# Soft-routed experts on one core: B22 loaded block by block, the second pair's reloads reordered, and the B11 sums moved in the program text

## The chip, the core and the metric

The kernel runs on one core of one Trainium2 chip. Its time is the device time of one execution in microseconds (us). The kernel before takes 1434.25 us, the median of 3 runs (1434.05 to 1435.16). The profile shown here is one further execution of the same program, with a span of 1434.2 us.

## What is computed

```python
batch, seq, hidden, n_experts, expert_hidden = 16, 512, 512, 8, 2048
probs = softmax(router_logits)                      # over the 8 experts
output = zeros(batch, seq, expert_hidden)
for e in range(8):
    output += probs[:, :, e:e+1] * (x @ expert_weights[e])
```

Every token goes through every expert, and the softmax of its logits weights the results. Written as one product, the output is Z times W: Z has 8192 rows (tokens) and 8 x 512 = 4096 columns, where column block e is x times the token's probability of expert e; W stacks the eight weight matrices to 4096 x 2048.

## The kernel before

The product Z W is cut into 2 x 2 blocks: token blocks of 256 rows are even or odd, experts are the first or the last four, output columns the first or the last 1024. Seven block products (numbered 1 to 7) then stand for eight, at the price of sums and differences of blocks, which VectorE makes. The weight blocks are B11, B12, B21 and B22, each of four tiles `w` of 128 x 4096 f16 (1 MB); the list `BLOCKS` names the four tiles. Products 1, 5, 2 and 4 are cut once more in the same way by `sub_product` (its seven inner products are the `prod(p, ...)` below, and its weights are the four tiles and the "inner sums" of them). Their results go to DRAM, product 4 into the output and products 1, 2 and 5 into `kept`. The last stage goes once over 16 pairs of row blocks (`for q in range(NI)`), makes products 6, 7 and 3, and reads `kept` back.

All helpers record their instructions on one line: L142 is every matmul of `mm`, L122 every two-operand VectorE operation of `tt`, L136 every DMA issued by GpSimd (`pool`), L133 every DMA issued by SyncE (`sp`). The program is written with a scheduling layer. It keeps VectorE and ScalarE instructions in the order of the text where `pinned[0]` is true; the others it may place elsewhere in their engine's order:

```python
    pinned = [True]
    def dve(i):
        note(i)
        if pinned[0]:
            tc.keep_in_program_order(i)
    def tt(o, a, b, op):
        dve(nc.vector.tensor_tensor(out=o, in0=a, in1=b, op=op))
```

The inner sums of a weight block are four operations on VectorE, each one tile from another:

```python
    def inner_sums(b, t3=None):
        t3 = t3 or b[0, 1]
        w = {1: b[0, 0], 2: b[1, 0], 3: b[1, 1], 7: t3}
        def step(p, x, y):
            if p not in w:
                w[p] = new_w()
            tt(w[p], x, y, SUB)
        return w, [lambda: step(5, b[0, 1], b[0, 0]), lambda: step(6, b[1, 1], w[5]),
                   lambda: step(4, w[6], b[1, 0]), lambda: step(7, b[1, 1], b[0, 1])]
```

The start of the kernel makes product 1 of the first row blocks directly (`z0`), and meanwhile the softmax of all tokens and the operands of the next two row blocks (numbers 4 and 6, `xp1`), whose probabilities are spread over the partitions by a matmul of `ones` with a diagonal matrix `d`:

```python
    def early_xp1(j, d):
        ...
        for c in range(C):
            mm(ps[:, ds(c * P, P)], xs0[:, j, ds(c * P, P)], ident, c == 0, c == C - 1)
        evacuate(xp1[t][0][:, :, rows], ps.rearrange("p (c t) -> p c t", c=C), 0)
        ps = bank()
        mm(ps, ones, d.rearrange("p e t -> p (e t)"), True, True)
        evacuate(xp1[t][1][:, :, rows], ps.rearrange("p (e t) -> p e t", e=HE), 1)
    ...
    for n in range(2):
        ps = [bank() for _ in range(4)]
        for e in range(HE):
            ...
            for c in range(C):
                for j in range(4):
                    mm(ps[j], z0[j][:, e, c], b11[e // 2, n][:, e % 2 * C + c, :],
                       e + c == 0, e == HE - 1 and c == C - 1)
            if n == 1:
                for j in ((4, 5), (6, 7), (), ())[e]:
                    early_xp1(j, ds_[j - 4])
                if e == 1:
                    sums[0]()
        for j in range(4):
            o = half()
            act(nc.scalar.copy(o, ps[j]))
            sp(kept[1][j // 2][n].rearrange("(p j) m -> j p m", j=2)[j % 2], o)
        if n == 0:
            ph0.append(early_p(1))
            softmax_of_all()
            ds_ = [diag_j(j) for j in range(4, 8)]
            w, sums = inner_sums(b11, new_w())
    ...
    pinned[0] = False
    sub_product(1, 0, P1, w, weights_of_t1(), 1,
                xp1, (sums[1], sums[3], sums[2]))
```

`sub_product` makes the operands of its first row blocks, then calls `rest`, then multiplies:

```python
            a11, a12 = (mul(*xp[0], e0, 2, 0, HQ) for e0 in (0, 2))
            a21, a22 = (mul(*xp[1], e0, 2, 0, HQ) for e0 in (0, 2))
            ...
            s1 = new(a21, a22, ADD)
            s2 = new(s1, a11, SUB)
            s4 = new(a12, s2, SUB)
            tt(a21, a11, a21, SUB)
            for make in rest:
                make()
            ...
                r1 = keep(prod(1, "x"))
                put(0, 0, prod(2, "b"), r1, ADD)
                r5 = keep(prod(5, "q"))
                r2 = keep(prod(6, "x", False))
                put(0, 1, prod(3, "q", False), r2, ADD)
                ...
```

The last stage, cut to the parts that the change touches:

```python
        def load_kept(self, j):
            tn = QUARTERS[j]
            self.m1[tn] = from_kept(1, self.q, *tn, "m")
            self.m5[tn] = from_kept(5, self.q, *tn, "v")
        def c11(self, j):
            tn = QUARTERS[j]
            m2 = from_kept(2, self.q, *tn, "m")
            tt(m2, self.m1[tn], m2, ADD)
            self.put(0, 0, tn, m2)
    ...
        xs, vs = [], []
        for j, tn in enumerate(QUARTERS):
            if j > 1:
                rows.load_kept(j)
            x = bank()
            act(nc.scalar.copy(x, rows.m1[tn]))
            if o10 and j == 0:
                o10()
            if j > 1 or q == 1:
                rows.c11(j)
            ...
            plain(x, 6, w6, tn, False)          # 16 matmuls onto the kept product 1
            v = half("u")
            tt(v, x, rows.m5[tn], ADD)
```

Here L626 is `act(nc.scalar.copy(x, rows.m1[tn]))`, and L595 is the GpSimd queue's store in `put`. `"m"` has five buffers, `"v"` four. The four tiles of B22 (`w3`) are needed by product 3 of q = 0, after 4 x 16 matmuls of product 6 and as many of product 7.

Of the kernel before, what the change touches and what calls it, by code (L numbers as in the profile page):

```python
# [32 lines left out]
def kernel(  # L33
# [38 lines left out]
    BLOCKS = ((0, 0), (1, 0), (0, 1), (1, 1))  # L72
# [41 lines left out]
# [4 lines that stand above are left out]
# [17 lines left out]
    def pool(o, i):  # L135
        note(nc.gpsimd.dma_start(out=o, in_=i))  # L136

    def bank():
        return psum.tile([P, NB], f32, name="ps", tag="ps")
# [8 lines left out]
    def new_w():  # L148
        return wpool.tile([P, K8, NB], f16, name="w", tag="w")

    def cast_w(q, kn, e, t, parts=1):
        k, n = kn
        for c in range(0, C, C // parts):
            pool(t[:, ds(e * C + c, C // parts), :],
                 expert_weights[(q // 10 - 1) * HE + 2 * k + e, ds(c * P, C * P // parts),
                                ds((q % 10 - 1) * NH + n * NB, NB)].rearrange("(c p) n -> p c n", p=P))

    def load(what, kn, gate=True):
        t = new_w()
        if gate:  # L160
            dve(nc.vector.memset(t.rearrange("p (e c) n -> p e c n", e=2)[:, :, 0, 0:2], 0.0))  # L161
        if (what, kn) in stored:
            pool(t, stored[what, kn])
        else:
            for e in range(2):
                cast_w(what, kn, e, t)
        return t
# [5 lines left out]
# [12 lines that stand above are left out]
    def inner_weights(b):  # L185
        w, sums = inner_sums(b)
        sums[0]()
        yield
        sums[1]()
        sums[2]()  # L190
        yield
        sums[3]()
        return w
# [72 lines left out]
    def diag_e(e):  # L266
        return diag(ph0[0][:, e].unsqueeze(2))
# [11 lines left out]
    xp1 = [[xpool.tile([P, C, HQ], f16, name=name, tag="x") for name in ("xT", "pT")] for t in range(2)]  # L279
# [73 lines left out]
    def half(use="any"):  # L353
        return h_tile([P, NB], f32, use)
# [87 lines left out]
# [3 lines that stand above are left out]
            if n == 0 and e < 2:  # L445
                early_z0(e + 2, ds_[e + 2])
                if e == 0:
                    ds_.append(diag_e(3))
# [4 lines that stand above are left out]
            if n == 1:  # L453
                for j in ((4, 5), (6, 7), (), ())[e]:
                    early_xp1(j, ds_[j - 4])
                if e == 1:
                    sums[0]()
        for j in range(4):
            o = half()
            act(nc.scalar.copy(o, ps[j]))  # L460
# [7 lines that stand above are left out]
    def weights_of_t1():  # L468
        b = {}
        for i, kn in enumerate(BLOCKS):  # L470
# [7 lines left out]
    x_new.extend((4 + 2 * t, xp1[t][0]) for t in range(2))  # L478
    share(xs=3, r=4, o=8)
    sub_product(1, 0, P1, w, weights_of_t1(), 1,  # L480
                xp1, (sums[1], sums[3], sums[2]))


    def weights_of_21():
# [31 lines left out]
    w6, w7, w3 = {}, {}, {}  # L516

    def weights_of_main():
        for kn in BLOCKS:
            t, w7[kn] = load(22, kn), load(12, kn)  # L520
            yield
            tt(w7[kn], t, w7[kn], SUB)
        for kn in BLOCKS:
            w6[kn] = load("t2", kn)
        yield
        w3.update({kn: load(22, kn, False) for kn in BLOCKS})
    share(r=4, o=11)
    sub_product(4, 1, P2, ready[4], weights_of_main())

# [67 lines left out]
    rows = Rows(0)  # L597
# [5 lines left out]
        rows.c11(j)  # L603
    pinned[0] = True
    o10 = None
    sums = inner_weights(w3)
    for q in range(NI):
        following = Rows(q + 1) if q + 1 < NI else None

        def ahead(make, k, following=following):  # L610
            if following:
                getattr(following, make)(k)

        def plain(ps, r, w, tn, start):
            t, n = tn
            for k in range(2 * K8):
                mm(ps, rows.z[r][k // K8][:, k % K8, ds(t * P, P)], w[k // K8, n][:, k % K8, :],
                   start, k == 2 * K8 - 1)


        xs, vs = [], []
        for j, tn in enumerate(QUARTERS):
            if j > 1:
                rows.load_kept(j)
            x = bank()
            act(nc.scalar.copy(x, rows.m1[tn]))  # L626
            if o10 and j == 0:
                o10()
            if j > 1 or q == 1:
                rows.c11(j)  # L630
            if j < 2:
                rows.s4(j)
            else:
                ahead("a11", j - 2)
            plain(x, 6, w6, tn, False)
            v = half("u")
            tt(v, x, rows.m5[tn], ADD)
            xs.append(x)
            vs.append(v)

        banks = {}

        def seeded(b, v, scale=1.0):
            banks[b] = bank()
            act(nc.scalar.mul(banks[b], v, scale))  # L645
        if q:
            seeded("b", vs[0])
            seeded("d", vs[3], -1.0)
            if q == NI - 1:
                seeded("e", vs[3], -1.0)  # L650
        else:
            seeded(0, vs[0])
            seeded(1, vs[1])


        if q == 1:
            inner3 = finish(sums)
        if q:
            z3 = rows.inner()
        for j, tn in enumerate(QUARTERS):  # L660
            x, m5 = xs[j], rows.m5[tn]
            plain(x, 7, w7, tn, False)
            c21 = half("m")
            act(nc.scalar.copy(c21, x))  # L664
            rows.put(1, 0, tn, c21, accum_op=ADD)
            tt(m5, x, m5, ADD)
            rows.put(1, 1, tn, m5)
            if j < 2:
                ahead("s2", j)


        def early(j):
            if following:
                following.load_kept(j)
                if q:
                    following.c11(j)

        ahead("s3", 0)
        if q == 0:
            def c12(j, tn, rows=rows, vs=vs, banks=banks):  # L680
                act(nc.scalar.copy(vs[j], banks[j]))
                rows.put(0, 1, tn, vs[j])

            for j, tn in enumerate(QUARTERS):
                plain(banks[j], 3, w3, tn, False)
                if j < 2:
                    seeded(j + 2, vs[j + 2])
                if j < 3:
                    c12(j, tn)
                if j < 2:  # L690
                    early(j)
                    next(sums)
            ahead("s3", 1)
            o10 = lambda: c12(3, QUARTERS[3])
            rows = following
            continue

        def prod(p, b):
            if b not in banks:
                banks[b] = bank()  # L700
            for k in range(K8):
                mm(banks[b], z3[p][:, k, :], inner3[p][:, k, :],
                   p in (1, 5) and k == 0, k == K8 - 1)
            return banks[b]

        def put(j, *args, rows=rows, vs=vs):
            tt(vs[j], *args)
            rows.put(0, 1, QUARTERS[j], vs[j])

        v00, v01, v11, v10 = vs  # L710
        x = prod(1, "x")
        r1 = half("r")
        act(nc.scalar.copy(r1, x))  # L713
        put(0, prod(2, "b"), r1, ADD)
        early(0)
        r5 = prod(5, "q")
        tt(v11, r5, v11, ADD)
        prod(6, "x")
        tt(v01, x, v01, ADD)
        early(1)  # L720
        put(1, prod(3, "q"), v01, ADD)
        prod(7, "x")
        r3 = half("r")
        act(nc.scalar.copy(r3, x))  # L724
        put(2, x, v11, ADD)
        ahead("s3", 1)
        if q < NI - 1:
            d = prod(4, "d")

            def o10(put=put, r3=r3, d=d):  # L730
                put(3, r3, d, SUB)
        rows = following
# [35 lines left out]
```

## Time and profile before

| | |
|---|---|
| time, median of 3 | 1434.25 us |
| span of the profiled execution | 1434.2 us |
| TensorE (PE) busy | 1424.9 us, 6654 matmuls, granted clock 0.999 |
| VectorE (DVE) busy | 1032.0 us, 72% |
| ScalarE (ACT) busy | 271.0 us, 19% |
| GpSimd (POOL) busy | 219.6 us, 15% |
| DMA | 318.92 MB, mean 222 GB/s |

In the lines of a trace the first number is a start in us from the span's beginning and the second a duration; `L142` is a line of the kernel. `ps<-w,z` names what is written and read. `x16` counts instructions merged into one line, and the brackets at a line's end give the engine's idle time just before it and what released it. `gap <- X` in a list of waits means that the engine stood still until X. A chain of waits is followed back from the last instruction to whatever released each step.

### The profile page before, as it was taken

What the parts mean: (1) busy time and instruction counts of PE and PEld (TensorE: products, weight loads), DVE (VectorE), ACT (ScalarE), POOL (GpSimd) and SP (SyncE); (2) the same over time, 40 slices, a digit from 0 to 9 for tenths busy, and PEclk for the clock granted to TensorE, in tenths of its full rate; (3) what the DMA queues carried; (4) which work ended last, traced back from release to release, by engine and by line L of the source; (5) the groups of instructions that cost most, each with busy time, mean ns of one, the idle gap of its engine ahead of it and who ended that gap; (6) DMA issues with size and microseconds to landing.
All of it is one profiled execution on the core that took longest, in us unless ns stands there. A gap on an engine that the chain in (4) does not pass through costs nothing.

```text
span 1434.2 us, 18172 instructions
## 1 busy us (share of the span) xinstructions
PE 1424.9 (99%) x6654; PEld 647.9 (45%) x6654; DVE 1032.0 (72%) x1173; ACT 271.0 (19%) x472; POOL 219.6 (15%) x344
## 2 busy tenths in 40 slices
PE   9999999999999999999999999999999999999998
PEld 4444444444444444444444444444444444444444
DVE  6967585656686867766767687777777877877773
ACT  3211111111111111111111211111111111111111
POOL 3111000110001000001000222222222222222220
PEclk9999999999999999999999999999999999999999
DMA  9899967899649994467766967777777767778764
GB/s 196 185 249 266 274 160 191 183 258 259 208 148 301 352 338 147 132 191 222 213 248 206 298 188 238 237 237 233 229 220 226 210 212 214 231 234 242 220 199 103
DMA packets 192041, 318.92 MB, mean 222 GB/s; under 512 B 51664, under 2 KB 80592, under 8 KB 187344
## 3 DMA queue, kind: packets, MB, share of 16 engines
q1 hardware_dynamic: 135328, 202.92, 44.2%
q0 software_dynamic: 56624, 114.84, 34.1%
q8 instruction: 52, 0.85, 0.2%
q14 instruction: 37, 0.30, 0.1%
HBM read 180.13 MB, written 159.58 MB: 237 GB/s over the span
## 4 chain that ended last, share of the span: by engine, by line
PE 93%; issue 3%; DMA 2%; POOL 1%; DVE 0%; ACT 0%; POOLq 0%; SPq 0%; DVEq 0%; ACTq 0%
PE ps L142 93%; POOL out_dram L595 1%; DMA h<-kept 1%; DMA out_dram<-h 1%; DMA w<-in_expert_weights_dram 1%; POOL w L136 0%; DVE z L122 0%; DVE h L122 0%; ACT ps L626 0%; SPq L133 0%; POOLq L595 0%; POOL ident L235 0%; DVEq L122 0%; POOLq L136 0%; POOLq L235 0%
## 5 line engine op out<-in xcount | busy, mean ns | idle before, releaser
L142 PE MATMUL ps<-w,z 128*128 128x512 f16 x6560 | 1415.2, 379 | 3.5 <-ACT ps L626 1.9
L142 PEld LDWEIGHTS <-z 128*128 128x128 f16 x6560 | 641.6, 98 | 776.0 <-issue 2.2
L122 DVE TENSOR_TENSOR h<-ps,h 128x512 f32<-128x512 f32 x389 | 267.7, 689 | 312.9 <-PE ps L142 89.2
L122 DVE TENSOR_TENSOR z<-xT,pT 128x2048 f16<-128x2048 f16 x252 | 304.2, 1218 | 32.5 <-PE ps L142 30.5
L122 DVE TENSOR_TENSOR z<-z 128x2048 f16<-128x2048 f16 x280 | 303.6, 1108 | 7.3
L404 ACT COPY h<-ps 128x512 f32<-128x512 f32 x248 | 145.3, 586 | 602.1 <-PE ps L142 594.9
L595 POOL DMA_DIRECT2D out_dram<-h x244 | 153.7, 663 | 535.4 <-DVE h L122 328.8
L122 DVE TENSOR_TENSOR w<-w 128x4096 f16<-128x4096 f16 x36 | 82.3, 2286 | 0.8 <-DMA w<-wd 0.7
L664 ACT COPY h<-ps 128x512 f32<-128x512 f32 x64 | 37.5, 585 | 177.0 <-PE ps L142 172.4
L136 POOL DMA_DIRECT2D h<-in_x_dram x30 | 21.3, 709 | 263.3 <-DMA xT<-h 226.2
L122 DVE TENSOR_TENSOR h<-h 128x512 f32<-128x512 f32 (+1 forms) x67 | 46.0, 687 | 20.8 <-DMA h<-kept 20.3
L122 DVE TENSOR_TENSOR h<-h,ps 128x512 f32<-128x512 f32 (+1 forms) x78 | 52.7, 675 | 11.0 <-PE ps L142 10.9
L136 POOL DMA_DIRECT2D w<-in_expert_weights_dram x41 | 30.8, 765 | 187.3 <-DVE w L161 131.0
L645 ACT ACTIVATE ps<-h 128x512 f32<-128x512 f32 x35 | 21.0, 602 | 166.9 <-DVE h L122 166.9
L626 ACT COPY ps<-h 128x512 f32<-128x512 f32 x64 | 35.6, 593 | 36.3 <-DMA h<-kept 30.7
L136 POOL DMA_DIRECT2D w<-wd x12 | 6.5, 543 | 189.1 <-DVE w L161 116.1
L724 ACT COPY h<-ps 128x512 f32<-128x512 f32 x15 | 8.8, 585 | 120.7 <-PE ps L142 120.7
L713 ACT COPY h<-ps 128x512 f32<-128x512 f32 x15 | 8.8, 586 | 16.5 <-PE ps L142 16.5
L260 DVE CAST z<-ps 128x512 f16<-128x512 f32 x8 | 5.2, 686 | 4.3 <-PE ps L142 4.3
L136 POOL DMA_DIRECT2D w<-wdt x8 | 4.4, 560 | 21.9 <-DVE w L161 21.9
L260 DVE CAST xT<-ps 128x512 f16<-128x512 f32 x4 | 2.6, 687 | 5.4 <-PE ps L142 5.4
L142 PEld LDWEIGHTS <-w 128*128 128x128 f16 x80 | 5.0, 98 | 2.6 <-DMA w<-in_x_dram 0.9
(37 smaller groups left out, 44.3 us busy)
## 6 DMA issues: line engine op xcount, KB each, us to landing
out_dram<-h POOLq DMA_DIRECT2D x244, 256.0 KB, 4.9
kept<-h SPq DMA_DIRECT2D x192, 256.0 KB, 4.1
h<-kept SPq DMA_DIRECT2D x192, 256.0 KB, 4.6
pT<-p_dram SPq DMA_DIRECT2D x124, 256.0 KB, 5.1
w<-in_expert_weights_dram POOLq DMA_DIRECT2D x39, 512.0 KB, 12.8
out_dram<-h SPq DMA_DIRECT2D x75, 256.0 KB, 3.4
xT<-x SPq DMA_DIRECT2D x62, 256.0 KB, 2.8
w<-wd POOLq DMA_DIRECT2D x12, 1024.0 KB, 10.7
```

Source lines behind the costliest of these rows:

```text
L122: dve(nc.vector.tensor_tensor(out=o, in0=a, in1=b, op=op))
L136: note(nc.gpsimd.dma_start(out=o, in_=i))
L142: nc.tensor.matmul(ps, z, w, start=start, stop=stop, skip_group_check=True)
L260: dve(nc.vector.tensor_copy(o, ps))
L404: nc.scalar.copy(t, ps)
L595: queue.dma_start(out=out_rows(self.q, odd, tn[0], cols, tn[1]), in_=o, **how)
L626: act(nc.scalar.copy(x, rows.m1[tn]))
L645: act(nc.scalar.mul(banks[b], v, scale))
L664: act(nc.scalar.copy(c21, x))
L713: act(nc.scalar.copy(r1, x))
L724: act(nc.scalar.copy(r3, x))
```

## The change

Three edits. First, the four sums of B11 are no longer called at two places (one inside the starting loop, three after the operands of `sub_product`) but all four in `sub_product`, in the text behind the operands of its first row blocks; the aim is that these operands don't wait for sums. Second, the four loads of B22 leave the end of product 4, where they were issued together as the buffers came free, and go to the quarters of q = 0 in the last stage: two at j = 1, one at j = 2, one at j = 3, each now gated by a small VectorE memset (`load` with its default gate). The aim is that the 4 MB don't compete in one burst with the reloads of `kept`. Third, in q = 1 the kept products 1 and 5 of quarters 2 and 3 are requested at j = 0, ahead of the kept product 2 that `c11` reads.

```diff
@@ the starting loop
             if n == 1:
                 for j in ((4, 5), (6, 7), (), ())[e]:
                     early_xp1(j, ds_[j - 4])
-                if e == 1:
-                    sums[0]()
@@ product 1
     sub_product(1, 0, P1, w, weights_of_t1(), 1,
-                xp1, (sums[1], sums[3], sums[2]))
+                xp1, [sums[i] for i in (0, 1, 3, 2)])
@@ weights_of_main, during product 4
         for kn in BLOCKS:
             w6[kn] = load("t2", kn)
         yield
-        w3.update({kn: load(22, kn, False) for kn in BLOCKS})
@@ the last stage
-    sums = inner_weights(w3)
     for q in range(NI):
...
         for j, tn in enumerate(QUARTERS):
-            if j > 1:
+            if j > 1 and q != 1:
                 rows.load_kept(j)
+            if q == 1 and j == 0:
+                rows.load_kept(2)
+                rows.load_kept(3)
             x = bank()
             act(nc.scalar.copy(x, rows.m1[tn]))
+            if q == 0 and j:
+                for kn in ((), BLOCKS[:2], BLOCKS[2:3], BLOCKS[3:])[j]:
+                    w3[kn] = load(22, kn)
             if o10 and j == 0:
                 o10()
...
         else:
             seeded(0, vs[0])
             seeded(1, vs[1])
+            sums = inner_weights(w3)
```

## The prediction

> **What bounds the kernel now.** I read the page's busy times first, then TensorE's waits, then the chain, and then the order in time around the stalls that these show. Of the page:
>
> ```profile
> PE 1424.9 (99%) x6654; PEld 647.9 (45%) x6654; DVE 1032.0 (72%) x1173; ACT 271.0 (19%) x472; POOL 219.6 (15%) x344
> L142 PE MATMUL ps<-w,z 128*128 128x512 f16 x6560 | 1415.2, 379 | 3.5 <-ACT ps L626 1.9
> ```
>
> TensorE is the bound: the 6560 large matmuls cover 1415.2 us, 0.2157 us each (the mean of 379 ns is longer because they overlap), and the granted clock of 0.999 leaves nothing to win there. The change alters no matmul. What it can move is only time in which TensorE stands still. The list of TensorE's waits names all of it:
>
> ```profile
> PE ps L142 <- ACT ps L626: 1.9, 1, 1.9
> PE ps L142 <- DMA w<-in_expert_weights_dram: 1.3, 1, 1.3
> PE ps L142 <- DVE z L122: 0.3, 1, 0.3
> ```
>
> The 1.3 us is the first weight tile, which the change leaves alone. The 0.3 us is at 48.49 us, where inner product 3 of `sub_product` waits for s4 on VectorE; from matmul to matmul it costs 0.5 us. The 1.9 us (2.0 from start to start) is at 844.81. Of the chain in order of time:
>
> ```profile
> 832.68 5.00 DMA out_dram<-h
> ...
> 838.13 5.96 DMA h<-kept
> ...
> 844.17 0.60 ACT ps L626
> 844.77 0.04 issue
> 844.81 585.53 PE ps L142 x2720
> ```
>
> At 844 the fourth quarter of q = 1 waits for its kept product 1, which SyncE could request only at 838.13, behind a reload of kept product 2 whose buffer an output store freed at 837.68. So the change can win at most 0.5 + 2.0 = 2.5 us. What it can lose has no such limit, so the start of the kernel needs a look. VectorE there, in order of time:
>
> ```profile
> 16.59 0.19 DVE L202 TENSOR_REDUCE h<-lg 128x4 f32<-128x32 f32 x1 [0.29 <-ACT lg L200]
> ...
> 19.31 0.69 DVE L202 TENSOR_REDUCE h<-h 128x64 f32<-128x512 f32 x1 [0.69 <-ACT h L200]
> 20.03 0.55 DVE L203 RECIPROCAL h<-h 128x64 f32<-128x64 f32 x1
> 20.62 1.54 DVE L122 TENSOR_TENSOR h<-h 128x512 f32<-128x512 f32 x2
> 22.07 2.49 DVE L122 TENSOR_TENSOR h<-ident,ph 128x512 f16<-128x512 f16 x4
> 29.39 1.29 DVE L260 CAST xT<-ps 128x512 f16<-128x512 f32 x2 [4.83 <-PE ps L142]
> 30.79 2.36 DVE L122 TENSOR_TENSOR z<-xT,pT 128x2048 f16<-128x2048 f16 x2
> 33.73 1.29 DVE L260 CAST xT<-ps 128x512 f16<-128x512 f32 x2 [0.58 <-PE ps L142]
> 34.93 2.28 DVE L122 TENSOR_TENSOR w<-w 128x4096 f16<-128x4096 f16 x1
> ```
>
> The softmaxes come first, then the four diagonal matrices (22.07 to 24.56). TensorE takes the first of these in the line below at 29.19, nearly 5 us after VectorE had the last one ready. The first sum of B11 (2.28 us) runs at 34.93, after everything that TensorE needs here.
>
> ```profile
> 28.97 0.39 PE L142 MATMUL ps<-ident,w 128*128 128x128 f16 x4
> 29.19 0.38 PE L142 MATMUL ps<-h,ones 128*128 128x512 f16 x1
> ```
>
> Last, GpSimd's load of the last half tile of B11, its line in time and what the answer on this tile says of its landing:
>
> ```profile
> 15.09 0.74 POOL L136 DMA_DIRECT2D w<-in_expert_weights_dram x1 [2.04 <-DMA w<-in_expert_weights_dram]
> DMA to landing us min/median/max: 18.6/18.6/18.6
> ```
>
> It lands at 33.7. The third tile's last half (issued at 7.3, 18.2 us to landing) lands at 25.5.
>
> **What the Trainium skill says.** "Perfetto Trace Analysis", section Tensor Engine Instruction, says that ScalarE, VectorE and GpSimd execute strictly first in, first out. So an operation that waits for a DMA holds back all behind it, ready or not. The trace agrees: VectorE's operations run in the order of the built program throughout these 50 us. "TensorE: Matmul & The Clock Gate", section What's actually happening, says that after an idle window of about 3.4 us the array falls to half its clock, and regains it after such a window of work. The kernel's first ten matmuls agree, 0.427 us apart against 0.216 later; what idling does in between no run shows yet, since TensorE's longest stall is 2.0 us. "VectorE: DVE Perf Modes", section The perf-mode tier table, gives a two-operand f16 operation of 2048 elements 1224 ns; the trace has 1.22 us for `z`, and 2.28 us for a sum of 4096.
>
> **Part 1, the sums of B11.** In the text all four now stand behind the operands of blocks 4 and 6. But they stand where `pinned[0]` is false, and the instruction before, which pinned the first one in place, is gone. The built program shows where the scheduling layer puts them. VectorE's order after the change, from the first softmax on (names shortened):
>
> ```
> TensorReduce (softmax of four tiles)
> w <- b11[0,1] - b11[0,0]        waits for the loads of both
> Reciprocal, multiply; reduce, subtract, reduce (softmax of all)
> w <- b11[1,1] - that sum        waits for both halves of b11[1,1]
> Reciprocal
> w <- b11[1,1] - b11[0,1]
> multiply (softmax of all)
> w <- sum - b11[1,0]
> add, then the four diagonal matrices, then the casts of xT
> ```
>
> So the sums move forward, into the softmaxes, and ahead of the diagonal matrices that TensorE waits for. TensorE's own order hardly changes: four transposes, two large matmuls (new here), then `ones` with the first diagonal. It gets there at 28.97 + 4 x 0.055 + 2 x 0.216 = 29.6.
>
> VectorE's path to that diagonal, with the durations above: first sum at 25.5 (third tile landed), done at 27.8, the reductions by about 31. The second sum waits for the landing at 33.7 and ends at 36.0. Then reciprocal 0.55, sum 2.28, multiplication 1.1, sum 2.28, addition 0.43, diagonal 0.69: 7.3 us, less some 0.3 because each operation starts about 0.05 to 0.08 before the one ahead ends. The diagonal is ready at 43.0. **TensorE stands still for 43.0 - 29.6 = 13.4 us.** Nothing else it could do is ahead in its order.
>
> After 13.4 us of idling the array should start at half clock. I take the ten slow matmuls at the kernel's start as the measure: 10 x (0.427 - 0.216) = 2.1 us.
>
> Behind this the operands are no longer slowed by sums. TensorE ends the starting loop 11.5 us after that diagonal (as now, 29.6 to 41.1) plus 2.1, at 56.6, and inner products 1, 2, 5 and 6 take 32 x 0.216 = 6.9 us more, to 63.5. VectorE goes through the casts and operands and ends s4 at about 59.5. So the 0.5 us at 48.49 go. The stores of the probabilities leave some 20 us later than now, but the next blocks' operands are needed only at about 81 and their reloads should land by 57.
>
> Part 1: +13.4 + 2.1 - 0.5 = **+15.0 us**.
>
> **Part 2, B22.** Now its four loads leave between 781 and 786 and take 7.0, 10.5, 11.9 and 13.3 us. No TensorE wait hangs on them directly. After the change two leave after quarter 0 of q = 0 (about 795 in the old times), the others at about 799 and 803 to 806. Product 3 needs the first two 28 us after the stage's start at 791, at 818.6, and the others at 822. Even at 13 us per load the last lands at 819. Four memsets of 0.06 us are hidden. **0 us**, and a shorter queue for the reloads.
>
> **Part 3, the order in q = 1.** In SyncE's order the product 1 tile of the last quarter moves up from the place now issued at 838.13 to the one now issued at 822.99, which landed in 5 us. It would be there at about 828, 14 us early. The 2.0 us go: **-2.0 us**. The product 2 tiles come later instead; that of the last quarter lands about 846 and holds VectorE to about 847, but what follows (sums and operands of product 3, some 6 us) is needed only at about 860.
>
> Sum: +15.0 - 2.0 = +13.0, so 1434.25 + 13.0 = **1447.2 us**.
>
> **Rivals.** (a) The change does what its text says: sums behind the operands, and both stalls gone: 1434.25 - 2.5 = 1431.7. For it speaks the source, against it the built order, and the trace of before, which followed its built order. (b) The stall comes, but the clock stays up or B11 lands earlier, since the probabilities' stores now leave after it: each us of earlier landing is a us less; with 32.5 and no cold start 1444. Against: that traffic is small. (c) The stall moves rather than goes in the last stage: late product 2 tiles hold VectorE in q = 1, or B22 comes late. For it speaks that VectorE must take product 2 in order; it would put back some 2 to 4 us, 1449 to 1451. (d) The delay starves the second round of `sub_product`, whose probabilities now leave at 42: a few us more. TensorE's own delay of 15 us speaks against it.
>
> **Range and chances.** The landing carries about 1 us each way, the chain of VectorE 0.5, the cold start 0 to 3.4, the last stage 0 to +3. Together 1443.5 to 1450.5. 2% slower would be 1462.9, twice the loss I find; 2% faster is below the time of the matmuls. So faster 0.01, same 0.97, slower 0.02.
>
> **What would show it.** Right: a wait of about 13 us of TensorE for VectorE near 30 us, on `ps<-h,ones` or its weight load; the second `w<-w` waiting for the DMA until about 33.7; some ten matmuls 0.427 apart behind it; no stall at inner product 3; none in q = 1. Wrong: `w<-w` after `z` in VectorE's line of time (rival a), a new stall about 15 us behind 820 or 860 (rival c), or idle matmuls near 80 to 100 (rival d).

## The result and the profile after

The changed kernel takes 1447.57 us (median of 4, 1447.24 to 1448.89) where the kernel before took 1434.7 beside it: 1.0089 times as long, with a 95% interval of 1.0071 to 1.0106. The prediction had 1447.2, in a range from 1443.5 to 1450.5.

The list of TensorE's waits, to be held against the one of before. Three entries are new or larger, three of before's are gone:

```profile
PE ps L142 <- DVE h L122: 10.7, 1, 10.7
PE ps L142 <- ACT h L458: 1.7, 1, 1.7
PE ps L142 <- DMA w<-in_x_dram: 1.4, 2, 0.9
```

The 0.3 us at s4 (`DVE z`) and the 1.9 us in q = 1 (`ACT ps`) are not there any more. The third that is gone, 1.3 us for the first weight tile, and the 1.4 us for `in_x_dram` both lie in the first 11 us, where the first inputs arrive at other times. The 10.7 us are a wait for one of VectorE's `h` tiles. TensorE in order of time shows for which:

```profile
29.71 0.38 PE L142 MATMUL ps<-ident,w 128*128 128x128 f16 x4 [1.70 <-ACT h L458]
29.93 0.59 PE L142 MATMUL ps<-w,z 128*128 128x512 f16 x2
41.22 0.61 PE L142 MATMUL ps<-h,ones 128*128 128x512 f16 x1 [10.70 <-DVE h L122]
```

It is the `ones` matmul with the first diagonal, at 41.22 instead of 29.19. VectorE in order of time says why it comes late (the brackets: idle time just before, and what ended it):

```profile
24.43 2.29 DVE L122 TENSOR_TENSOR w<-w 128x4096 f16<-128x4096 f16 x1 [8.16 <-DMA w<-in_expert_weights_dram]
...
29.12 0.69 DVE L202 TENSOR_REDUCE h<-h 128x64 f32<-128x512 f32 x1 [0.69 <-ACT h L200]
32.16 2.29 DVE L122 TENSOR_TENSOR w<-w 128x4096 f16<-128x4096 f16 x1 [2.35 <-DMA w<-in_expert_weights_dram]
34.37 0.55 DVE L203 RECIPROCAL h<-h 128x64 f32<-128x64 f32 x1
34.83 2.23 DVE L122 TENSOR_TENSOR w<-w 128x4096 f16<-128x4096 f16 x1
36.97 1.06 DVE L122 TENSOR_TENSOR h<-h 128x512 f32<-128x512 f32 x1
37.95 2.28 DVE L122 TENSOR_TENSOR w<-w 128x4096 f16<-128x4096 f16 x1
40.15 0.42 DVE L122 TENSOR_TENSOR h<-h 128x256 f16<-128x256 f32 x1
40.48 2.49 DVE L122 TENSOR_TENSOR h<-ident,ph 128x512 f16<-128x512 f16 x4
```

The four `w<-w` are the sums of B11. Two of them wait for loads, 8.16 and 2.35 us, in the middle of the softmaxes; in the kernel before all of this came after the diagonals. The chain of waits, which in the kernel before ran through output stores and reloads around 780 to 844, now is this one path and then TensorE to the end:

```profile
13.95 18.11 DMA w<-in_expert_weights_dram
...
32.16 2.29 DVE w L122
34.45 0.46 DVE h L203
...
36.97 1.06 DVE h L122
38.03 2.20 DVE w L122
40.23 0.95 DVE h L122 x2
41.18 0.05 issue
41.22 1400.08 PE ps L142 x6494
```

After 41.22 TensorE waits for nothing more in this execution; what is left is a lower clock up to 45.1, which an experiment below takes up.

### The profile page after: what moved, and what is told of

Read it like the earlier page. It is cut to its first block, busy times and chain, and to the rows that moved or that the text cites. A ratio compares the mean times of both kernels' runs of the same rounds, so it can differ in the third digit from the quotient of the medians.

```text
span 1445.2 us, 18174 instructions
## 1 busy us (share of the span) xinstructions
PE 1426.0 (99%) x6654; PEld 648.4 (45%) x6654; DVE 1032.6 (71%) x1177; ACT 271.4 (19%) x472; POOL 219.7 (15%) x344
## 4 chain that ended last, share of the span: by engine, by line
PE 97%; DMA 2%; DVE 1%; issue 0%; POOL 0%; POOLq 0%; DVEq 0%
PE ps L142 97%; DMA w<-in_expert_weights_dram 2%; DVE w L122 0%; POOL w L136 0%; DVE h L122 0%; DVE h L203 0%; POOL ident L235 0%; POOLq L235 0%; DVEq L122 0%; POOLq L755 0%
## 5 line engine op out<-in xcount | busy, mean ns | idle before, releaser
L142 PE MATMUL ps<-h,ones 128*128 128x512 f16 x4 | 2.0, 500 | 10.7 <-DVE h L122 10.7
```

The costliest lines, as they stand in the source:

```text
L142: nc.tensor.matmul(ps, z, w, start=start, stop=stop, skip_group_check=True)
```

## The experiments

### Each part alone

**The sums alone**, in the kernel before:

```diff
-                if e == 1:
-                    sums[0]()
-                xp1, (sums[1], sums[3], sums[2]))
+                xp1, [sums[i] for i in (0, 1, 3, 2)])
```

> The kernel before with the four B11 sums moved as in the change, and nothing else. If the sums ahead of the diagonals are the whole loss, this is slower than the kernel after by the 2.0 us that its last stage keeps losing at q = 1: about 1449.5 us, 14.8 over before, with waits of TensorE for ScalarE (about 1.7 us) and VectorE (about 11 us) near 30 to 41 us and some ten matmuls 0.427 us apart behind them. If instead the B22 loads or the reordered reloads cost time that the sums' stall hides in the sum, this is faster than after, below 1447.

Measured: 1448.87 us (median of 4), 1.0103 times before (1.0088 to 1.0119). Before had 1434.05 in these runs (median of 33), so the sums alone cost 14.8 us. The waits are those of after, and no other part is needed for the loss:

```profile
PE ps L142 <- DVE h L122: 10.5, 1, 10.5
PE ps L142 <- ACT h L458: 2.2, 1, 2.2
```

One detail missed: the stall at q = 1 that I carried over from before was only 0.2 us in this trace. So the 1.3 us over the kernel after (2.0 expected) are not that stall here; in the two traces they lie at the start, where the first diagonal came at 42.77 instead of 41.17.

**B22 alone**, spread over q = 0 (`sums = inner_weights(w3)` also moves, as in the change):

```diff
-        w3.update({kn: load(22, kn, False) for kn in BLOCKS})
...
+            if q == 0 and j:
+                for kn in ((), BLOCKS[:2], BLOCKS[2:3], BLOCKS[3:])[j]:
+                    w3[kn] = load(22, kn)
```

> The kernel before with the B22 loads gated and spread over q = 0, and nothing else. My theory says that the order of the reloads makes the stall at the fourth quarter of q = 1: then it stays, 1434.7 us within 0.7, with TensorE waiting about 2 us for ScalarE near 844. The rival, that the burst of 4 MB makes the reloads late, says the stall goes: about 1432.7.

Measured: 1434.32 us (median of 13), 1.0004 times before (0.9995 to 1.0012). The stall stays:

```profile
PE ps L142 <- ACT ps L624: 1.5, 1, 1.5
```

That is the copy of the kept product 1 in the fourth quarter of q = 1, at 843.6. So the burst of B22 loads did not cause it.

**The reloads alone:**

```diff
-            if j > 1:
+            if j > 1 and q != 1:
                 rows.load_kept(j)
+            if q == 1 and j == 0:
+                rows.load_kept(2)
+                rows.load_kept(3)
```

> The kernel before with the kept products 1 and 5 of q = 1 requested ahead of product 2, and nothing else. My theory: the 2.0 us stall at q = 1 goes, about 1432.7 us, no wait of TensorE for ScalarE longer than 0.5 us in the last stage. The rival, that the burst of B22 loads is the cause, says the stall stays: 1434.7.

Measured: 1433.59 us (median of 13), 0.9996 times before (0.9988 to 1.0004). The trace shows no wait of TensorE in the last stage: the order of the reloads does remove the stall. All eight traces of kernels with the new order, those below included, lack it, and all five with the old order have it, from 0.2 to 2.3 us in the lists of waits. But by the medians this is worth about 0.5 us, a quarter of the expected 2.0, and the interval includes no gain at all.

**Both, without the sums** (the two diffs above together):

> The change without its sums: B22 spread and the reloads reordered. Both theories: the stall at q = 1 goes, 1432.7 us, 2.0 under before; the start is that of before, with the 0.5 us at inner product 3. If the two together delay the product 2 tiles so that VectorE comes late, some of the 2 us comes back near 850 to 860.

Measured: 1433.68 us (median of 13), 0.9996 times before (0.9988 to 1.0004), again without a wait in the last stage. The two parts don't disturb each other, and they don't add up to more than the reloads alone.

### How large is the stall in q = 1?

Where did 1.5 of the 2.0 us go? Two more traces of the kernel before, unchanged:

> The kernel before itself, for a second trace. The reordered reloads won only 0.4 us by the medians where I had read a 2.0 us stall. If that stall varies from execution to execution, this trace shows another size of it, with the reload of the fourth quarter's product 1 landing at another time; if it is fixed, it shows 2.0 us again and the gain went elsewhere.

> The kernel before a third time. As for the second trace: a size of the stall at q = 1 between 0 and 2 us if it varies, 2.0 if it is fixed.

Their lists of TensorE's waits, the second trace and then the third (in these files every line number is one higher):

```profile
PE ps L143 <- ACT ps L627: 0.8, 1, 0.8
```

```profile
PE ps L143 <- ACT ps L627: 2.3, 1, 2.3
```

From matmul to matmul the stall was 2.0, 1.0 and 2.4 us in the three traces. The reload was requested at 838.13, 837.76 and 837.74 and took 6.0, 4.7 and 6.1 us to land; ScalarE needs some 0.7 us to copy it, and TensorE wanted the copy at 842.2 to 842.8. So the stall is the tail of one DMA. In the third trace it costs more than itself. The table of stretches around it (PEclk is the third number from the right):

```profile
842.00:845.40 3.40, 1.13 (x6) 0.45 (x5) 2.08 (x3) 1.12 (x2) 0.40 (x1) 1.00 0.69 254
845.50:848.80 3.30, 3.30 (x9) 1.18 (x8) 0.34 (x1) 0.00 (x0) 0.04 (x1) 0.50 0.53 159
848.90:852.00 3.10, 3.10 (x16) 1.45 (x15) 2.00 (x2) 0.60 (x1) 0.00 (x0) 1.00 0.25 82
```

The clock stood at half from 845.5 to 848.9, and eight matmuls started 0.43 us apart: 1.7 us on top of the 2.4. Neither of the other two traces has such a stretch. The three executions took 1435.99, 1434.36 and 1437.47 us. The times of the other runs fit: the 33 runs of before beside them range from 1433.22 to 1437.22, the 13 runs with B22 alone from 1433.18 to 1437.13, but the 13 with the reloads alone only from 1432.97 to 1434.10. The new order mostly cuts off this tail; the means differ by 0.55 us (1434.19 and 1433.64), hardly more than the medians. Without their stalls, and without the slow matmuls of the third, the three traced executions would have taken 1434.0, 1433.4 and 1433.3 us, near the 1433.59 of the reloads alone: by this estimate a median execution of before, at 1434.05, stands still for about half a microsecond there. How the stall is spread over the runs without a trace is not measured.

### Is the stall at the start the landing of a load?

In the kernel after, the last B11 tile is loaded ahead of the token blocks 4 and 6:

```diff
-    cast_x(4)
-    cast_x(6)
     for e in range(2):
         cast_w(11, BLOCKS[3], e, b11[BLOCKS[3]])
+    cast_x(4)
+    cast_x(6)
```

> The kernel after with the last tile of B11 loaded ahead of the token blocks 4 and 6 (2.7 us of transfers). If the wait of the second sum for this tile is part of the stall, the tile lands about 2.6 us earlier and the stall shrinks by the 2.35 us that VectorE waited: about 1445.3 us, the first diagonal at about 39. If VectorE's own work sets the stall, it stays at 1447.6.

Measured: 1445.59 us (median of 4), 2.0 under after, 1.0082 times before (1.0066 to 1.0097). Each held against the kernel before beside it (1434.7 and 1433.98), the gain is 1.3. The wait of the second sum shrinks from 2.35 to 1.17 us:

```profile
30.20 2.29 DVE L122 TENSOR_TENSOR w<-w 128x4096 f16<-128x4096 f16 x1 [1.17 <-DMA w<-in_expert_weights_dram]
32.41 0.68 DVE L202 TENSOR_REDUCE h<-h 128x64 f32<-128x512 f32 x1
```

The tile landed at 30.11 instead of 32.06. The scheduling layer then put this sum ahead of a reduction (the second line), which adds 0.7 us behind the landing. So the landing is part of the path, but not all of it: a wait of 8.2 us for the diagonal was left. (TensorE also waited 2.8 us for the token blocks, which now come behind the tile. That costs nothing, since the diagonal was later still.) A second trace of the kernel after tells how the rest behaves:

> The kernel after, for a second trace: the first diagonal should come 9.1 to 9.4 us after the landing of the last B11 half tile whenever that lands, and TensorE should have no wait in the last stage.

This execution took 1448.18 us. The last half tile landed at 32.85 and the first diagonal ended at 41.96, 9.11 us later; in the first trace it was 32.06 and 41.17, also 9.11, and with the sums alone 33.66 and 42.77, 9.11 again. From the landing on, the path is a fixed row of VectorE operations. The other half of the expectation missed: in this trace TensorE also waited 0.5 us for a VectorE result at 880.9, late in q = 1, which the first trace didn't have. On the chain of that trace a reload of kept product 2 was requested at 857.69 and landed at 862.06, and VectorE's operations from there on lead to this result: the new order of the reloads has a price of its own, small and not in every execution.

### Does idling cost clock?

In the kernel after, 46 extra matmuls fill the wait, into a bank that the `ones` matmul then overwrites:

```diff
+        if j == 4:
+            for _ in range(46):
+                mm(ps, ones, xs0[:, 0, :], True, True)
         mm(ps, ones, d.rearrange("p e t -> p (e t)"), True, True)
```

> The kernel after with 46 extra matmuls (9.9 us of work whose result is overwritten) between the transposes of the first of these blocks and the matmul that waits for the diagonal. They fit into the wait. If idling puts the array to half clock, the nine matmuls 0.427 us apart become 0.216 us apart and 1.9 us go: about 1445.7 us. If these slow steps have another cause, the time stays at 1447.6 and the slow steps too.

Measured: 1445.89 us (median of 4), 1.7 under after, 1.0082 times before (1.0068 to 1.0096): a kernel with 46 more matmuls is faster. Each held against the kernel before beside it, the gain is 1.0; that it is no earlier landing shows in the trace, where the first diagonal came 0.6 us later than in after's. The table of stretches shows the reason in its column PEclk, the granted clock; first the kernel after, then the filled one:

```profile
29.00:41.00 12.00, 0.81 (x6) 0.35 (x6) 9.53 (x8) 2.74 (x7) 0.72 (x1) 0.60 0.79 178
41.00:45.00 4.00, 3.78 (x12) 1.61 (x13) 3.90 (x7) 1.17 (x2) 0.00 (x0) 0.50 0.50 87
```

```profile
29.00:41.00 12.00, 10.47 (x50) 4.80 (x51) 8.97 (x8) 3.27 (x7) 0.71 (x1) 1.00 0.77 175
41.00:45.00 4.00, 3.15 (x17) 1.48 (x17) 3.90 (x8) 1.17 (x2) 0.00 (x0) 1.00 0.61 102
```

Idle, the clock fell to 0.5 (at 31.47) and stayed there for the first 4 us of work. After that idling the large matmuls start 0.427 us apart; in the filled kernel they start 0.216 apart.

### Sums where the text has them

The operands of blocks 4 and 6 and the four sums of the kernel after, pinned:

```diff
+            pinned[0] = bool(rest)
             a11, a12 = (mul(*xp[0], e0, 2, 0, HQ) for e0 in (0, 2))
...
             for make in rest:
                 make()
             rest = ()
+            pinned[0] = False
```

> The kernel after with the operands of blocks 4 and 6 and the four sums pinned in the order in which the text has them, so that the sums really stand behind the operands. The diagonals come at 24 us again and the 11 us wait and the cold matmuls go. But inner product 5 then needs the first sum, which by the durations of before ends at 46.8 where TensorE wants it at 44.6, and inner product 6 the second at 49.0: about 2.7 us of stall in place of before's 0.5. With the 2.0 us won at q = 1: about 1434.9 us. The rival, that sums behind the operands cost nothing, says 1432.2.

Measured: 1436.53 us (median of 21), 1.0018 times before (1.0012 to 1.0025). The long wait and the cold matmuls are gone, but so is the gain that the text promised. TensorE's list of waits now has

```profile
PE ps L142 <- DVE w L122: 2.1, 1, 2.1
...
PE ps L142 <- ACT h L406: 0.7, 1, 0.7
```

The first is inner product 5 waiting for the first sum, 2.3 us from matmul to matmul at 45.7. The second follows at 48.3 and costs 0.8: a matmul waits for ScalarE's copy of the result of inner product 5 (L406), not inner product 6 for the second sum as expected, for that sum was still running (46.19 to 48.48). That is 3.1 us of stall (expected 2.7) in place of 0.5. The traced execution took 1435.72 us, 1.74 over the median of before beside it (1433.98): the 2.6 us more of stall, less the gain in the last stage, which is again nearer to 0.5 than to 2.0. The median is higher for another reason, which no trace shows. Of the 21 runs, ten from 1435.49 to 1436.47 have a mean granted clock of 1.000 and eleven from 1436.53 to 1437.98 one of 0.999, as it would be if a stretch of half clock like the one in the third trace of before, with its 1.7 us, often followed these stalls.

### A version that beats both

The last stage of the change, the first sum where before had it, and s4 pinned ahead of the operand s3 and of the sums for inner products 7 and 4:

```diff
-            s4 = new(a12, s2, SUB)
-            tt(a21, a11, a21, SUB)
-            for make in rest:
-                make()
+            if rest:
+                rest[0]()
+            pinned[0] = bool(rest)
+            s4 = new(a12, s2, SUB)
+            tt(a21, a11, a21, SUB)
+            for make in rest[1:]:
+                make()
             rest = ()
+            pinned[0] = False
```

> B22 spread and reloads reordered, the first sum where before had it, and the operand s4 pinned ahead of s3 and of the two last sums. By before's durations s4 then ends at 45.2 where inner product 3 wants it at 48.0, the sums for inner products 7 and 4 end at 48.6 and 50.8 where they are wanted at 49.7 and 51.5. So the 0.5 us stall goes too: about 1432.2 us, 2.5 under before. If another operand takes its place, 1432.7.

Measured: 1432.78 us (median of 21), 0.999 times before (0.9984 to 0.9997), 0.9 under the same kernel without the pinned operands (1433.68; 0.5 was expected). TensorE waits for nothing after the first 9 us. Its complete list:

```profile
PE every L104 <- DVE h L101: 1.3, 1, 1.3
PE ps L142 <- DMA w<-in_x_dram: 0.6, 1, 0.6
PE ps L142 <- DVE lg L303: 0.3, 1, 0.3
```

## Why the prediction was right, step by step

**The sums move forward: right.** VectorE followed the order of the built program to the last instruction of this stretch, and rival (a), which trusted the source, was 16 us off.

**The stall, 13.4 us: 12.7 measured.** The first diagonal was ready at 41.17, not 43.0. The B11 half tile landed at 32.06 in this trace instead of 33.67, which is 1.6 of the 1.8 us; the path behind it took 9.11 us where I had 9.3. The stall is shorter by only 0.7, because TensorE too was early: in this execution the first weights came sooner, its matmuls before the transposes ended 1.1 us earlier, and it would have reached the `ones` matmul at 28.5, not 29.6. In the trace the stall has two parts. 1.9 us of it (start to start) come already at the transposes, which wait for a bank: ScalarE copies that bank out only after the exponential of the softmax, which itself waited 12.4 us for VectorE. I had not seen this second way in which the delay reaches TensorE. It cost nothing extra, since the diagonal was later still.

**The cold start, 2.1 us: 1.9 measured** from the steps in the trace, 1.7 by the filled kernel. The measure that I took, the ten slow matmuls at the kernel's beginning, held. This agrees with the half clock of the Trainium skill, "TensorE: Matmul & The Clock Gate", section What's actually happening; its busy window of about 3.4 us compares with 4.1 us at half clock here (41.22 to 45.30).

**The 0.5 us at inner product 3: right**, its wait is gone. **B22: right**, 0 us: the last load landed at 826.17, some 9 us before product 3 wants that tile (822 in the old times, and this stage stands 13.0 us later). The experiment alone gives a ratio of 1.0004.

**The reloads, -2.0 us: mechanism right, size wrong.** The reload of the fourth quarter moved up to 836.95 and landed at 842.17, that is 829.2 in the old times (predicted: 828), and the wait is gone. But I took the size of the stall from a single execution, and one that was 1.7 us slower than the median. The medians give 0.5 us for it, with an interval that includes zero.

**The sum.** In the traces the sums cost 12.7 + 1.9 - 0.5 = 14.1 us, against +15.0 predicted and 14.8 measured with the sums alone. That the total of 1447.2 lies within 0.4 us of the median is partly luck: two terms were too large in opposite directions, the loss by 0.2 to 0.9 and the gain by about 1.5, and the same program ranged from 1447.24 to 1448.89. Rival (d) did not come true. Rival (c) did in part: the tile of kept product 2 landed as predicted (VectorE waited for it until 859.84, that is 846.8 in the old times), but the margin behind it was thin, and in the second trace it cost the 0.5 us at 880.9.

## What to carry to other kernels

Where a scheduling layer may move instructions, read the built order and not the text: removing one pinned call let four operations run ahead of what the bound engine was waiting for. An operation that depends on a load holds back everything behind it on an engine that runs in order, so such an operation belongs behind the last result that the bound engine needs before that load has landed, and, as the pinned variant showed, not behind more than that. The size of a stall that is the tail of one DMA should be read from several traces before it enters a sum.

## What was not expected of the hardware

A stall well under the 3.4 us idle window of "TensorE: Matmul & The Clock Gate", section What's actually happening, can cost the clock. In the third trace of before 2.4 us of idling were followed by 3.4 us at half clock. With the sums alone, the clock fell at 31.85, at the end of a window in which TensorE had idled 2.4 us and had just worked again; stalls of 2.0 us in the first trace of before, 1.6 us with B22 alone and 2.3 us in the pinned kernel did not lower it. The length of a stall does not decide alone: in the long wait of the changed kernel it fell 1.1 us after TensorE had gone idle in the first trace (31.47), and 3.5 us after that in the second (34.65).

The stretches at half clock have a common length. They last 3.41 us (845.46 to 848.88 in the third trace of before), 10.24 us (34.65 to 44.89 in the second trace of after) or 13.65 us (31.47 to 45.12 in the first): once, three and four times 3.41. I cut the thirteen traces into pieces of 3.41 us from their first change of clock on. From full, the clock fell at the end of every piece in which TensorE was busy for 1.40 us or less, and of none in which it was busy for 1.51 us or more. The two pieces nearest to this border, from the end of the first trace of before (the clock fell at 1432.34) and from the second trace of after (it did not fall at 31.24), then the two pieces over which the 2.3 us of the pinned kernel are spread (the second number is TensorE's busy time):

```profile
1428.93:1432.34 3.41, 1.40 (x13) 1.00 (x11) 1.44 (x3) 0.27 (x1) 0.00 (x0) 1.00 0.50 177
27.82:31.24 3.42, 1.51 (x10) 0.52 (x8) 2.06 (x4) 1.97 (x5) 0.71 (x1) 1.00 1.24 206
41.75:45.16 3.41, 1.89 (x9) 0.69 (x7) 3.41 (x3) 0.59 (x1) 0.00 (x0) 1.00 0.32 59
45.16:48.57 3.41, 2.16 (x10) 0.94 (x11) 3.41 (x4) 0.58 (x1) 0.71 (x1) 1.00 0.79 120
```

In the third trace of before the 2.4 us lay in one piece (842.05 to 845.46), with 1.14 us of work. The busy times rest on matmul ends that the profiler models, so the border is an estimate.
